# Two steps of a streaming-encoder layer joined: attention's transposes with its value products, and the scan's output products with the next chunk's first ones

## The chip, the cores and the metric

The kernel runs on one core of a Trainium2 chip. The metric is the device time of one execution in microseconds (us). Every run here is of the same program with the same inputs; a smaller time is better.

## The reference

One hybrid layer over 2048 frames of width 1024 (with 16 meta tokens ahead of them). One projection of `h` feeds two token mixers; their outputs are gated, projected, merged and normalised.

```python
(q_a, k_a, v_a, z_a, beta_a, dec_a, q_b, k_b, v_b, z_b, gate_a, gate_b) = jnp.split(h @ w_in, offsets, axis=-1)
# A: gated delta rule, a scan over chunks
v_new = u_c - w_c @ S
o_c = q_c @ S + attn_c @ v_new
S = S * gl_c + k_c.T @ v_new
# B: sliding-window attention with sinks and meta tokens, 16 heads on 4 key-value heads
scores = einsum('bkgncd,bknsd->bkgncs', q, k_w) * (SWA_HD ** -0.5) - slopes * dist
probs = softmax(concatenate([scores, sink], axis=-1), axis=-1)[..., :-1]
o = einsum('bkgncs,bknsd->bkgncd', probs, v_w)
# both are multiplied by silu(z), projected, merged with sigmoid gates, and projected again
mixed = g_a * (y_a @ w_proj_a) + g_b * (y_b @ w_proj_b)
out = layer_norm(ALPHA * h + mixed @ w_out)
```

## The kernel before, in words

The sequence is cut into four blocks of 512 frames, and `block(b)` builds the program of each. The large products are in `proj` (L311): one unit multiplies 128 rows of a weight with the block's 512 columns in 24 matmuls, because weight and input are split into a high and a low part. Every six of these matmuls the generator `proj` yields, and that is one tick.

The order of the program is written by these generators. `run(fill, streams, rates)` walks through the units; at each tick it first calls `tick()`, which issues the delayed endings that `bg` has put aside for so many ticks, and then takes at most one step of each stream whose due amount has reached 1. A rate of 1.20 therefore means one step at each tick, and 0.90 means a step at nine of ten ticks. One stream, `chain`, holds the scan of the delta rule (`stage_c` of four head pairs) and then the attention, `swa()`. The other, `side`, prepares the scan. Each engine gets its instructions in the order in which Python issues them and works them off in that order; a wait holds up all that stands behind it on that engine. The scheduler is not asked (`manual_schedule`).

The attention of a block has 16 iterations: four key-value heads by four column groups of 128 frames (two chunks each). Iteration i issues, in steps of the stream:

- `swa_front` (scores, L1105 on TensorE, 8 matmuls) of iteration i + 1; VectorE reads the scores from PSUM at L1107, two ticks later ScalarE takes exponentials (L1117), three ticks after that VectorE scales them (L1121, L1122, L1126)
- `swa_turn(0)`: four transposes of the first chunk's probabilities (L1140); ScalarE copies them out as the high part (L1142), and one tick later VectorE makes the low part (L1147)
- `late()` of iteration i - 1: `swa_vals(1)`, the four value products of the second chunk (L1156, twice L1158, L1159), and `swa_out`: ScalarE copies one half of the result out (L1164), VectorE adds the other (L1165) and multiplies it with the gate (L1169, twice)
- `swa_turn(1)`: the transposes of the second chunk
- `swa_vals(0)`: the value products of the first chunk. L1156 and L1159 read the high part, L1158 reads the low part of L1147

Each of these is a step of its own, so six large matmuls of `proj` stand between any two of them. When the last column group of a head is done, the head's result is split again (L1176 on ScalarE, L146 on VectorE). The gate and branch units of `proj` that run meanwhile have endings on VectorE too: L732 (the gate path's SiLU), L1047 (the low part of a query), L1250 (a gate times a branch).

In `stage_c` a chunk's output product (L960) is issued by a delayed ending, two ticks after the chunk's last step; the next chunk begins with L971. Products there go on with L979, L981 and L992, and VectorE's L974, L984 and L994 stand between them. L1023 is a transpose of the scan's result.

Of the kernel before, what the change touches and what calls it, by code (L numbers as in the profile page):

```python
# [15 lines left out]
AF = mybir.ActivationFunctionType  # L16
ALU = mybir.AluOpType
AX = mybir.AxisListType

P = 128  # L20
# [4 lines left out]
NC4 = TB // P  # L25
# [18 lines left out]

GS = (26, 9)
NG = 6
RATES = (0.45, 0.45, 0.45, 0.50, 1.20)
SIDE = (0.60, 0.50, 0.50, 0.55, 0.35)


# [25 lines left out]
def hybrid_kernel(  # L76
# [26 lines left out]
    V, A, G, T, SY = nc.vector, nc.scalar, nc.gpsimd, nc.tensor, nc.sync  # L103
# [26 lines left out]
    def s2(shape, dt=F32):  # L130
        return sp.tile(shape, dt, tag="s", name=nm("s"))
# [6 lines left out]
    def bank(pool=None):  # L138
        if pool is None:
            return pp.tile([P, 512], F32, tag="ps", name=nm("ps"))  # L140
        return pool.tile([P, 512], F32, tag="acc", name=nm("acc"))
# [81 lines left out]
    def until(cond):  # L223
        while not cond():
            yield
# [379 lines left out]
    def block(b, nextx):  # L605
# [337 lines left out]
        def stage_c(g):  # L943

            d, h0 = gr[g], 2 * g
            yield from until(lambda: "T" in d and "vtok" in d)
            kT, qT, ktok, vtok, attn, LT = (d[n] for n in ("kT", "qT", "ktok", "vtok", "attn", "LT"))
            sq, cj, ce = (d[n] for n in ("sq", "cj", "ce"))
            eg, neg = gates["eg"], gates["neg"]
            if first:  # L950
                yield from until(lambda: ("S", g) in meta)

            o = vtok
            so = tiny([P, 2, NC4], "so")

            def out(c, wd):
                yield 2
                pks = bank()
                for hh in range(2):
                    T.matmul(pks[:, hh * P:hh * P + P], attn[:, hh, c, :], wd[:, 0, hh, :], start=True, stop=True)  # L960
                yield 2
                V.tensor_tensor(out=o[:, :, c, :], in0=pks[:, 0:256].rearrange("p (h d) -> p h d", h=2), in1=o[:, :, c, :], op=ALU.add)
                yield 1
                for hh in range(2):
                    A.activation(junk, o[:, hh, c, :], AF.Square, accum_out=so[:, hh, c:c + 1])
                d["so", c] = True

            for c in range(NC4):
                pks = bank()
                for hh in range(2):  # L970
                    T.matmul(pks[:, hh * P:hh * P + P], kT[:, hh, c * P:(c + 1) * P], S[g][:, hh, :], start=True, stop=True)  # L971
                R = s2([P, 2, P])
                for hh in range(2):
                    V.scalar_tensor_tensor(out=R[:, hh, :], in0=pks[:, hh * P:hh * P + P], scalar=neg[:, c, h0 + hh:h0 + hh + 1],  # L974
                                           in1=vtok[:, hh, c, :], op0=ALU.mult, op1=ALU.add)
                yield
                pw = bank()
                for hh in range(2):
                    T.matmul(pw[:, hh * P:hh * P + P], LT[:, hh * NC4 + c, :], R[:, hh, :], start=True, stop=True)  # L979
                for hh in range(2):  # L980
                    T.matmul(pks[:, 256 + hh * P:256 + hh * P + P], qT[:, hh, c * P:(c + 1) * P], S[g][:, hh, :], start=True, stop=True)  # L981
                wd = s2([P, 2, 2, P])
                for hh in range(2):
                    V.tensor_scalar(out=wd[:, 1, hh, :], in0=pw[:, hh * P:hh * P + P], scalar1=ce[:, hh, c:c + 1], scalar2=None, op0=ALU.mult)  # L984
                for hh in range(2):
                    A.activation(wd[:, 0, hh, :], pw[:, hh * P:hh * P + P], AF.Copy, scale=cj[:, hh, c:c + 1])
                for hh in range(2):
                    A.activation(o[:, hh, c, :], pks[:, 256 + hh * P:256 + hh * P + P], AF.Copy, scale=eg[:, 0, c, h0 + hh:h0 + hh + 1])
                yield
                pu = bank()  # L990
                for hh in range(2):
                    T.matmul(pu[:, hh * P:hh * P + P], ktok[:, hh, c, :], wd[:, 1, hh, :], start=True, stop=True)  # L992
                for hh in range(2):
                    V.scalar_tensor_tensor(out=S[g][:, hh, :], in0=S[g][:, hh, :], scalar=eg[:, 2, c, h0 + hh:h0 + hh + 1],  # L994
                                           in1=pu[:, hh * P:hh * P + P], op0=ALU.mult, op1=ALU.add)
                bg(out(c, wd))
                yield

            def end():
                yield lambda: ("so", NC4 - 1) in d  # L1000
                V.scalar_tensor_tensor(out=so, in0=so, scalar=1.0 / P, in1=sq, op0=ALU.mult, op1=ALU.add)
                ro = tiny([P, 2, NC4], "ro")
                rsqrt_small(ro, so, [P, 2, NC4], "rs")
                for hh in range(2):
                    for c in range(NC4):
                        V.tensor_scalar(out=o[:, hh, c, :], in0=o[:, hh, c, :], scalar1=ro[:, hh, c:c + 1], scalar2=None, op0=ALU.mult)
                yield 1
                d["o"] = o
                yield from stage_y(g)

            bg(end(), 1)
# [181 lines left out]
        def swa():  # L1193

            yield from until(lambda: ("q", 1) in sr[0] and len(ld) == 2)
            swa_bias(0, ld[0][3])
            nxt = swa_front(*seqn[0], *ld.pop(0))
            yield
            late = None
            for i, (kv, cp2) in enumerate(seqn):  # L1200
                w = nxt
                if i + 2 < len(seqn):
                    ld.append(swa_load(*seqn[i + 2]))
                if i + 1 < len(seqn):
                    k2 = seqn[i + 1][0]
                    yield from until(lambda: ("q", 1) in sr[k2])
                    swa_bias(k2, ld[0][3])
                    nxt = swa_front(*seqn[i + 1], *ld.pop(0))
                    yield
                yield from until(lambda: w["n"])  # L1210
                swa_turn(0, w)
                yield
                if late is not None:
                    late()
                    yield
                swa_turn(1, w)
                yield
                yield from until(lambda: ("p", 0) in w and ("ok", "zs", 1) in sr[kv])
                w["pO"] = bank()
                swa_vals(0, w)  # L1220
                yield

                def late(kv=kv, cp2=cp2, w=w):
                    swa_vals(1, w)
                    swa_out(kv, cp2, w)

            yield from until(lambda: ("p", 1) in w)
            late()
            yield
# [298 lines left out]
```

## Time and profile before

| what | value |
|---|---|
| median of 3 runs | 2648.5 us (2647.66 to 2649.97) |
| profiled execution, its own time | 2648.3 us |
| its span, first to last instruction | 2646.5 us |
| TensorE matmul busy (PE) | 2608.6 us, 99% |
| VectorE (DVE) / ScalarE (ACT) / GpSimd (POOL) busy | 58% / 46% / 29% |
| mean granted TensorE clock | 0.998 |

The busy time of an engine is the time in which at least one of its instructions runs; for TensorE matmuls overlap, so the distance from one start to the next says what a matmul costs, and not its duration. PEld is TensorE's loading of weights, which lies beside the matmuls. The granted clock is the share of full speed that the chip's throttle allows: 1.00 is 2.4 GHz, 0.50 is 1.2 GHz. A row of the timeline has its start in us, how long it took, the engine, the line, the operation, out<-in, and how many instructions are merged; in square brackets stands how long the engine was idle before it, and who ended that.

### The profile page before, as it was taken

Reading aid. Unit: us, or ns where it says so; the run is one execution under the profiler, and the core shown is the slowest. Engines: PE = TensorE matmul, PEld = TensorE weight load, DVE = VectorE, ACT = ScalarE, POOL = GpSimd, SP = SyncE. Lnnn points to the kernel's source line nnn. Section 1 sums busy time; section 2 is a strip of 40 time slices with the busy share of each in tenths; the row PEclk is TensorE's granted clock in tenths of the full one; section 3 lists DMA queues with packets and bytes.
Section 4 is the critical chain, followed back from the end, with each engine's and each line's share of the span. In section 5 each row is a group of like instructions: output and inputs, shape, how many; then the busy total and the mean of one; then the engine's idle time right before and its main releaser. Section 6 shows DMA issues by size and latency. Waiting matters only on the chain.

```text
span 2646.5 us, 44333 instructions
## 1 busy us (share of the span) xinstructions
PE 2608.6 (99%) x15444; PEld 2173.8 (82%) x15444; DVE 1533.4 (58%) x3863; ACT 1222.9 (46%) x3260; POOL 772.8 (29%) x1792
## 2 busy tenths in 40 slices
PE   9999999999999999999999999999999999999998
PEld 7677878888888888888888888888888888888886
DVE  6667756763565554763465554676347456476435
ACT  4565545552245544653224554565323454365422
POOL 2554333532056330111116532010102753011022
PEclk9999999999999999999999999999999999999999
DMA  7655555653675454674466545476347644557533
GB/s 257 207 198 180 186 191 159 200 167 96 205 244 169 135 167 143 201 207 132 152 225 186 170 135 164 151 212 184 120 157 243 190 142 149 164 172 210 171 98 136
DMA packets 243136, 461.61 MB, mean 174 GB/s; under 512 B 77648, under 2 KB 135760, under 8 KB 242912
## 3 DMA queue, kind: packets, MB, share of 16 engines
q1 hardware_dynamic: 242912, 458.78, 54.4%
q8 instruction: 122, 2.00, 0.3%
q14 instruction: 102, 0.84, 0.1%
HBM read 379.87 MB, written 78.81 MB: 173 GB/s over the span
## 4 chain that ended last, share of the span: by engine, by line
PE 89%; DVE 6%; ACT 3%; DMA 1%; issue 1%; SPq 0%; POOL 0%; DVEq 0%; ACTq 0%
PE acc L311 63%; PE ps L1140 2%; PE ps L1105 2%; PE ps L915 1%; PE ps L960 1%; PE ps L807 1%; PE ps L971 1%; PE ps L1158 1%; PE ps L992 1%; PE acc L1408 1%; PE acc L1411 1%; PE acc L1410 1%; PE ps L979 1%; PE ps L981 1%; PE ps L1408 1%; PE ps L1411 1%
## 5 line engine op out<-in xcount | busy, mean ns | idle before, releaser
L311 PE MATMUL acc<-xh,wh 128*128 128x512 f32 x1800 | 735.2, 408 | 0.3 <-ACT wh L275 0.3
L311 PE MATMUL acc<-xl,wh 128*128 128x512 f32 x1800 | 705.4, 392 | 0.0
L311 PE MATMUL acc<-xh,wl 128*128 128x512 f32 x1800 | 480.7, 397 | 0.0
L275 ACT ACTIVATE wh<-wr 128x1024 fp32r<-128x1024 f32 (+1 forms) x246 | 258.4, 1050 | 281.6 <-PE acc L311 151.8
L311 PEld LDWEIGHTS acc<-xh,wh 128*128 128x128 f32 x1800 | 339.1, 188 | 60.1 <-issue 1.4
L311 PEld LDWEIGHTS acc<-xl,wh 128*128 128x128 f32 x1800 | 339.7, 189 | 57.1
L311 PEld LDWEIGHTS acc<-xh,wl 128*128 128x128 f32 x1800 | 329.1, 189 | 65.6 <-issue 0.5
L718 DVE SCALAR_TENSOR_TENSOR s<-st,cw,s 128x512 f32<-128x512 f32 x288 | 229.4, 797 | 108.2 <-ACT st L713 101.2
L311 PE MATMUL acc<-y,wh 128*128 128x512 f32 x1024 | 251.5, 392 | 0.0
L146 DVE TENSOR_TENSOR wl<-wr,wh 128x1024 fp32r<-128x1024 f32 (+2 forms) x125 | 161.9, 1295 | 149.7 <-ACT wh L275 128.6
L841 POOL TENSOR_TENSOR tm<-X,g 128x60 f32<-128x60 f32 (+24 forms) x496 | 163.1, 329 | 251.8 <-DMA g<-d 216.7
L311 PEld LDWEIGHTS acc<-y,wh 128*128 128x128 f32 x1024 | 188.5, 188 | 36.7
L311 PE MATMUL acc<-xh,wr 128*128 128x512 f32 x624 | 210.7, 402 | 0.0
L1257 POOL TENSOR_TENSOR g<-g 128x512 f32<-128x512 f32 x32 | 69.7, 2177 | 395.4 <-DVE g L1250 385.5
L843 POOL TENSOR_TENSOR X<-X,tm 128x60 f32<-128x60 f32 (+24 forms) x496 | 170.8, 344 | 38.8
L1142 ACT ACTIVATE s<-ps 104x512 fp32r<-104x512 f32 (+2 forms) x128 | 76.3, 597 | 153.3 <-PE ps L1140 137.3
L1250 DVE SCALAR_TENSOR_TENSOR g<-g,acc 128x512 f32<-128x512 f32 x64 | 44.0, 687 | 154.5 <-PE acc L311 154.5
L311 PEld LDWEIGHTS acc<-xh,wr 128*128 128x128 f32 x624 | 115.6, 188 | 21.5
L311 PE MATMUL acc<-y,wl 128*128 128x512 f32 x512 | 130.7, 392 | 0.0
L146 POOL TENSOR_TENSOR wl<-wr,wh 128x256 fp32r<-128x256 f32 x120 | 87.0, 756 | 137.4 <-ACT wh L275 116.6
L760 POOL TENSOR_TENSOR g<-cm,gh 128x256 fp32r<-128x256 f32 x64 | 53.9, 872 | 249.6 <-DVE gh L672 206.9
L1241 ACT ACTIVATE g<-acc,bg__162 128x512 f32<-128x512 f32 x64 | 44.1, 689 | 177.3 <-PE acc L311 171.0
(340 smaller groups left out, 4679.6 us busy)
## 6 DMA issues: line engine op xcount, KB each, us to landing
wr<-in_wfm_dram SPq DMA_DIRECT2D x214, 512.0 KB
wl<-ws SPq DMA_DIRECT2D x165, 512.0 KB
wr<-ws SPq DMA_DIRECT2D x78, 512.0 KB
wh<-ws SPq DMA_DIRECT2D x75, 512.0 KB
ws<-wl SPq DMA_DIRECT2D x68, 512.0 KB
g<-kd SPq DMA_DIRECT2D x240, 96.0 KB
ws<-wh SPq DMA_DIRECT2D x38, 512.0 KB
wr<-in_wo_dram SPq DMA_DIRECT2D x32, 512.0 KB
```

The source lines that it names most:

```text
L146: eng.tensor_tensor(out=out_, in0=src, in1=f(hi), op=ALU.subtract)
L275: A.activation(hi[:, k], raw[:, k], AF.Copy)
L311: T.matmul(ps, w_[:, k, :], r_(k), start=(n == 0), stop=(n == 3 * NK - 1))
L718: V.scalar_tensor_tensor(out=acc, in0=st[:, 3 - d:TB + 3 - d], scalar=cw[:, s, 3 - d:4 - d], in1=acc, op0=ALU.mult, op1=ALU.add)
L760: G.tensor_tensor(out=gt[:, hh, c:c + 2], in0=tri.unsqueeze(1).to_broadcast([P, 2, P]), in1=part[:, c:c + 2, h0 + hh:h0 + hh + 1].to_broad ...
L841: G.tensor_tensor(out=tm[:, :n, :r], in0=X[:, :n, j:j + 1].to_broadcast([P, n, r]), in1=L[:, j:j + 1, j + 1:].to_broadcast([P, n, r]), op= ...
L843: G.tensor_tensor(out=X[:, :n, j + 1:], in0=X[:, :n, j + 1:], in1=tm[:, :n, :r], op=ALU.add)
L1105: T.matmul(o_, d["q", rt][:, 2 * cp2 + ch], KX[:, l, ch, s:208], start=l == 0, stop=l == 1)
L1140: T.transpose(out=pT[0:kt, j * 256 + rt * P:j * 256 + rt * P + P], in_=Pt[:, ch, rt, s + j * kt:s + j * kt + kt], identity=ident)
L1142: A.activation(ph[0:kt], pT[0:kt], AF.Copy)
L1257: G.tensor_tensor(out=m[:, u % 2, :], in0=t[:, 0, :], in1=t[:, 1, :], op=ALU.add)
L1408: T.matmul(acc, ah, wl[:, k2, :], start=False, stop=kq == 3 and k2 == 1)
```

## The change

Four things are edited. In `swa()`, `late()` no longer yields on either side: it follows `swa_turn(0)` in the same step. `swa_turn(1)` moves behind the wait for the first chunk's low part and into the step of `swa_vals(0)`. An iteration so has three steps instead of five. The rate of `chain` in the stage in which attention runs goes from 1.20 to 0.90. And in `stage_c` the output product of chunk c - 1 is issued right behind chunk c's first products instead of two ticks after the chunk's last step; what VectorE and ScalarE do with it stays in a delayed ending.

```diff
-RATES = (0.45, 0.45, 0.45, 0.50, 1.20)
+RATES = (0.45, 0.45, 0.45, 0.50, 0.90)
...
             def out(c, wd):
-                yield 2
-                pks = bank()
+                po = bank()
                 for hh in range(2):
-                    T.matmul(pks[:, hh * P:hh * P + P], attn[:, hh, c, :], wd[:, 0, hh, :], start=True, stop=True)
-                yield 2
-                V.tensor_tensor(out=o[:, :, c, :], in0=pks[:, 0:256].rearrange("p (h d) -> p h d", h=2), in1=o[:, :, c, :], op=ALU.add)
-                yield 1
-                for hh in range(2):
-                    A.activation(junk, o[:, hh, c, :], AF.Square, accum_out=so[:, hh, c:c + 1])
-                d["so", c] = True
-
+                    T.matmul(po[:, hh * P:hh * P + P], attn[:, hh, c, :], wd[:, 0, hh, :], start=True, stop=True)
+
+                def end():
+                    yield 2
+                    V.tensor_tensor(out=o[:, :, c, :], in0=po[:, 0:256].rearrange("p (h d) -> p h d", h=2), in1=o[:, :, c, :], op=ALU.add)
+                    yield 1
+                    for hh in range(2):
+                        A.activation(junk, o[:, hh, c, :], AF.Square, accum_out=so[:, hh, c:c + 1])
+                    d["so", c] = True
+
+                bg(end())
+
+            wd = None
             for c in range(NC4):
                 pks = bank()
                 for hh in range(2):
                     T.matmul(pks[:, hh * P:hh * P + P], kT[:, hh, c * P:(c + 1) * P], S[g][:, hh, :], start=True, stop=True)
+                if c:
+                    out(c - 1, wd)
                 R = s2([P, 2, P])
...
-                bg(out(c, wd))
                 yield
+            out(NC4 - 1, wd)
...
                 swa_turn(0, w)
-                yield
                 if late is not None:
                     late()
-                    yield
-                swa_turn(1, w)
                 yield
                 yield from until(lambda: ("p", 0) in w and ("ok", "zs", 1) in sr[kv])
+                swa_turn(1, w)
                 w["pO"] = bank()
                 swa_vals(0, w)
                 yield
```

The new lines shift the numbers: behind `stage_c` a line of the kernel before has a number that is six higher in the changed one (L1140 is L1146 there, L1147 is L1153, L1156 to L1159 are L1162 to L1165, L1164 is L1170, L1165 is L1171, L1169 is L1175). An iteration of the second block on TensorE, before; `cm` is the identity of a transpose, `acc` the bank of a large product, and the L1156 to L1159 in the middle write `ps_12068`, the bank of the iteration before:

```order
L1140 MATMUL ps_12135<-cm,g_11970 104x128 x4
L311 MATMUL acc_12148<-xh_7832,wh_12036 128x512
...
L1156 MATMUL ps_12068<-s_12058,s_10885 128x4x64
L1158 MATMUL ps_12068<-s_12066,s_10885 64x4x64 x2
L1159 MATMUL ps_12068<-s_12058,s_10885 128x4x64
L311 MATMUL acc_12148<-xh_7870,wh_12036 128x512
...
L1140 MATMUL ps_12181<-cm,g_11970 104x128 x4
L311 MATMUL acc_12148<-xh_7950,wh_12036 128x512
...
L1156 MATMUL ps_12196<-s_12140,s_11780 128x4x64
L1158 MATMUL ps_12196<-s_12164,s_11780 64x4x64 x2
```

The same iteration on TensorE in the changed kernel, where `s_12162` and `s_12179` are the high and the low part of the transposes in `ps_12157`:

```order
L1146 MATMUL ps_12157<-cm,g_11998 104x128 x4
L1162 MATMUL ps_12066<-s_12064,s_10885 128x4x64
L1164 MATMUL ps_12066<-s_12077,s_10885 64x4x64 x2
L1165 MATMUL ps_12066<-s_12064,s_10885 128x4x64
L311 MATMUL acc_12137<-xh_7870,wh_12019 128x512
...
L311 MATMUL acc_12137<-xl_7907,wh_12019 128x512
L1146 MATMUL ps_12181<-cm,g_11998 104x128 x4
L1162 MATMUL ps_12188<-s_12162,s_11804 128x4x64
L1164 MATMUL ps_12188<-s_12179,s_11804 64x4x64 x2
L1165 MATMUL ps_12188<-s_12162,s_11804 128x4x64
```

From the first transposes to the product that reads their low part there were three gaps of six large matmuls; one gap is left. VectorE in the same iteration, before; `s_12164` is the low part of the first chunk's transposes, `s_12170` the sum of the iteration before:

```order
L1047 SCALAR_TENSOR_TENSOR g_12131<-acc_12040,g_12131 64x8x64 x2
L1147 TENSOR_TENSOR s_12164<-ps_12135,s_12140 104x512
L1165 TENSOR_TENSOR s_12170<-ps_12068,s_12170 64x512
L1169 TENSOR_TENSOR g_11202<-s_12170,g_11202 64x2x128 x2
L1147 TENSOR_TENSOR s_12194<-ps_12181,s_12186 104x512
```

And VectorE in the changed kernel, with the first chunk's low part in `s_12179`:

```order
L1053 SCALAR_TENSOR_TENSOR g_12125<-acc_12023,g_12125 64x8x64 x2
L1171 TENSOR_TENSOR s_12168<-ps_12066,s_12168 64x512
L1175 TENSOR_TENSOR g_11202<-s_12168,g_11202 64x2x128 x2
L1153 TENSOR_TENSOR s_12179<-ps_12157,s_12162 104x512
L1153 TENSOR_TENSOR s_12199<-ps_12181,s_12186 104x512
```

The sum and the two gate products of the iteration before now stand ahead of the first chunk's low part on VectorE. In the scan, the first place on TensorE where the order differs (first block; - is before, + the change):

```order
-L960 MATMUL ps_2251<-s_2160,g_915 128x128 x2
 L311 MATMUL acc_2238<-xh_116,wh_2136 128x512
 L311 MATMUL acc_2238<-xl_117,wh_2136 128x512
...
-L971 MATMUL ps_2289<-S_85,g_565 128x128 x2
-L791 MATMUL ps_2295<-cm,g_2287 128x128 x4
+L975 MATMUL ps_2286<-S_85,g_565 128x128 x2
+L959 MATMUL ps_2289<-s_2160,g_915 128x128 x2
```

The output product of the first chunk (L960, L959 in the change) moved behind the second chunk's first product.

## Rows read from the trace of the kernel before

**Rows 1.** The page: busy us by engine, then the chain that ended last.
```profile
PE 2608.6 (99%) x15444; PEld 2173.8 (82%) x15444; DVE 1533.4 (58%) x3863; ACT 1222.9 (46%) x3260; POOL 772.8 (29%) x1792
...
PE 89%; DVE 6%; ACT 3%; DMA 1%; issue 1%; SPq 0%; POOL 0%; DVEq 0%; ACTq 0%
```
**Rows 2.** Windows: pure projection, then the second block's attention; clock behind POOL.
```profile
600.00:670.00 70.00, 70.00 (x310) 57.96 (x310) 26.20 (x26) 18.95 (x20) 14.74 (x7) 1.00 0.37 121
1068.00:1204.00 136.00, 135.35 (x756) 114.59 (x755) 95.15 (x301) 81.26 (x205) 15.40 (x70) 1.00 0.67 200
```
**Rows 3.** Waits of TensorE: us in total, times, longest.
```profile
PE ps L992 <- DVE s L984: 3.1, 3, 1.0
PE ps L1158 <- DVE s L1147: 2.6, 5, 1.6
...
PE ps L1140 <- DVE g L1126: 1.4, 5, 0.3
...
PE ps L1023 <- DVE s L1147: 1.1, 3, 0.4
```
**Rows 4.** Timeline of one attention iteration in the second block.
```profile
1127.86 0.39 PE L311 MATMUL acc<-xl,wh 128*128 128x512 f32 x1
...
1128.09 0.60 PE L1140 MATMUL ps<-cm,g 128*104 128x128 f32 x4
...
1128.73 0.60 ACT L1142 ACTIVATE s<-ps 104x512 fp32r<-104x512 f32 x1 [3.91 <-PE ps L1140]
1128.77 0.39 PE L311 MATMUL acc<-xl,wh 128*128 128x512 f32 x1
...
1129.92 0.28 PE L1156 MATMUL ps<-s,s 104*128 104x256 f32 x1
1130.04 0.40 PE L1158 MATMUL ps<-s,s 104*64 104x256 f32 x2
1130.27 0.28 PE L1159 MATMUL ps<-s,s 104*128 104x256 f32 x1
1130.39 0.40 PE L311 MATMUL acc<-xh,wh 128*128 128x512 f32 x1
...
1131.25 0.60 ACT L1164 ACTIVATE s<-ps 64x512 f32<-64x512 f32 x1
...
1131.79 0.60 PE L1140 MATMUL ps<-cm,g 128*104 128x128 f32 x4
1131.88 0.68 DVE L1165 TENSOR_TENSOR s<-ps,s 64x512 f32<-64x512 f32 x1 [1.60 <-ACT s L1164]
...
1132.60 0.85 DVE L1169 TENSOR_TENSOR g<-s,g 64x256 f32<-64x256 f32 x2
...
1133.48 0.69 DVE L1147 TENSOR_TENSOR s<-ps,s 104x512 fp32r<-104x512 f32 x1
...
1139.95 0.28 PE L1159 MATMUL ps<-s,s 104*128 104x256 f32 x1
```
**Rows 5.** VectorE's other work in this stretch, groups by line.
```profile
L146 DVE TENSOR_TENSOR y<-g,y 128x1024 fp32r<-128x1024 f32 x48 | 59.0, 1229 | 4.4 <-PE ps L1140 3.8 <-ACT wh L275 0.4
L1047 DVE SCALAR_TENSOR_TENSOR g<-acc,g 64x512 fp32r<-64x512 f32 x64 | 44.1, 690 | 17.7 <-ACT g L1043 16.5
L1250 DVE SCALAR_TENSOR_TENSOR g<-g,acc 128x512 f32<-128x512 f32 x64 | 44.0, 687 | 154.5 <-PE acc L311 154.5
```
**Rows 6.** Timeline of the first block's first iteration, a window behind it, one in the scan.
```profile
432.96 0.68 DVE L1147 TENSOR_TENSOR s<-ps,s 40x512 fp32r<-40x512 f32 x1
...
433.70 0.59 PE L1158 MATMUL ps<-s,s 40*64 40x256 f32 x2 [1.62 <-DVE s L1147]
...
434.43 2.93 PE L311 MATMUL acc<-xh,wl 128*128 128x512 f32 x6
...
434.00:435.00 1.00, 1.00 (x4) 0.70 (x3) 0.83 (x6) 0.00 (x0) 0.20 (x2) 0.50 1.07 360
...
908.00:912.00 4.00, 2.96 (x16) 2.21 (x15) 2.96 (x6) 1.60 (x5) 0.00 (x0) 1.00 0.40 133
```

## The prediction, made before the changed kernel ran

> **What bounds the kernel now.** I read the page first: TensorE is busy for 2608.6 of the span of 2646.5 us, and 89% of the chain that ended last is its own [rows 1]. The reader is to see that time can change in two ways only: TensorE gets other work, or it waits more or less. The change leaves the number of instructions alone, so only waits count. The next view, the stretch of the second block's attention, shows how little there is to win there: TensorE is busy for 135.35 of 136.00 us, VectorE for 95.15 and ScalarE for 81.26 [rows 2]. The list of TensorE's waits says the same: L1158 waits 2.6 us in total for L1147, L1140 1.4, L1023 1.1 for L1147, and L992 in the scan 3.1 [rows 3].
>
> The last view is one iteration, row by row [rows 4]. Three gaps of six large matmuls hide the chain of small steps between TensorE, ScalarE and VectorE there; that is why hardly anything waits.
>
> **The steps joined in attention.** What lies between the transposes and the product that reads their low part? In the kernel before, VectorE makes the low part (L1147) ahead of the sum and the gate products of the iteration before (L1165, L1169), and TensorE has three gaps to pass. In the change it makes it behind them, and TensorE has one gap. I set the need against the cover, both from T, the start of the last value product of the iteration before (L1159, at 1130.27 in [rows 4]).
>
> The cover, what TensorE does until it stands at L1158: 0.12 us to the next large matmul (1130.27 to 1130.39), 1.40 us for six of them (to the transposes at 1131.79), 0.44 us for four transposes and 0.12 us from L1156 to L1158 (1129.92 to 1130.04). The 0.44 us come from 1127.86 to 1128.77: 0.91 us for two large matmuls at 0.23 us each with four transposes between them, so 0.45, and I take 0.44. Sum: T + 2.08 us.
>
> The need: L1159 ends at T + 0.28, so ScalarE can take L1164 at T + 0.31. It has the copy L1142 of the new transposes ahead of it; this starts 0.64 us behind the transposes' start (1128.09 to 1128.73) and takes 0.60, and the transposes start 0.79 us ahead of T (0.44 for themselves, 0.35 from 1129.92 to 1130.27). So L1142 ends at T + 0.45, and L1164 starts between T + 0.31 and T + 0.47. From there the very sequence that the change sets up already stands in the trace once: L1164 at 1131.25, L1165 at 1131.88, L1169 at 1132.60, L1147 at 1133.48 with 0.69 us, so 2.92 us without a wait inside [rows 4]. TensorE then goes on 0.06 us later: L1147 ended at 433.64, L1158 started at 433.70 [rows 6]. Sum: T + 3.29 to T + 3.45.
>
> TensorE thus waits 1.21 to 1.37 us at L1158; I take 1.30. Of the 15 iterations of a block that have a predecessor, the order of the changed kernel leaves one gap of six in 14, and two gaps in one, where 1.40 us more cover it. 4 blocks x 14 x 1.30 = **73 us** (68 to 77).
>
> **What else stands ahead of L1147.** In three iterations of a block the split of a finished head (L146, 1.23 us) and in one or two another ending (L1250 or L732, about 0.69 us) now stand between L1169 and L1147 on VectorE [rows 5]. They add to the wait: 4 x (3 x 1.23 + 1.5 x 0.69) = **19 us**; at the low end half of it, 9, where VectorE gets to them in time. In two early iterations of a block a pair of L1047 (2 x 0.69 us) and the scaling of the next scores stand ahead of L1165: 0 to 8 us, I take **4**.
>
> **What the waits do to the clock.** In the first block's first iteration L1158 waited 1.62 us for L1147. Right behind it the granted clock was 0.50, that is 1.2 GHz, and six large matmuls took 2.93 us [rows 6] where 1.40 to the next kind is usual [rows 4]. So a long wait can cost about 1.5 us more. The longest wait of the scan, 1.0 us at L992 [rows 3], lies in the window from 908 to 912 us, and there the clock stays at 1.00 [rows 6]. Of the new waits those with L146 in them, 12 at 2.5 us, are longer than 1.62 us. I charge half of them: **10 us** (0 to 18). The Trainium skill ("Perfetto Trace Analysis", section "Matmul Optimizations") says that the matmul engine scales its power with utilization, and that matmuls should therefore run back to back in batches. By it, a step that joins two small groups should do no harm; the trace agrees on the first half only, with the 2.93 us behind a wait.
>
> **What comes back.** The waits at L1158, L1140 and L1023 (2.6 + 1.4 + 1.1 us) may go, with the 1.5 us of the one slow stretch, 6.6 us at most. The first iteration, where most of it lies, has no predecessor and keeps two gaps; I take **-3**. The joined groups save a change of shape 128 times; from 0.45 us for four inserted transposes against 4 x 0.11, that is 0.01 us each, **-1**.
>
> **At no cost.** The rate: before, 1.20 already meant one step per tick, so the steps slow down by a tenth but are three instead of five. Attention has 384 large matmuls among it per block and not 492, and the 108 others (25 us) follow behind. There TensorE runs without a pause, 70.00 of 70.00 us [rows 2], so moving them costs nothing; if cover were lacking there, its price would be that of the attention stretch. The keys' loads are issued one iteration ahead; an iteration lasts 9.68 us now (1130.27 to 1139.95 in [rows 4]) and in the forecast 9.68 - 7 x 0.23 + 1.3 = 9.4, so the lead stays; no row of L1105 waits for a transfer now [rows 3]. In the scan the output product moves behind L971 within the same tick or the next. It gives L974 0.45 us more cover and takes as much from L994, where nothing waits today; the price lies within the 3.1 us of L992, plus or minus, and I take 0.
>
> **The sum.** 73 + 19 + 4 + 10 - 3 - 1 = 102 us. The profiled execution took 2648.3 us (median of the three runs: 2648.5), so **2750 us**.
>
> **The rivals.**
> - *The clock falls at nearly every wait.* For it: the row at 434.43. Against it: waits of 1.0 us did nothing. 56 x 1.5 us in place of 10 give 74 more: 2825 us.
> - *A smaller loss.* If only about half of the iterations have to wait, because ScalarE and VectorE are ahead there, 28 x 1.30 + 9: 2690 us. Against it: the chain starts from TensorE's own L1159, so nothing can be ahead of it.
> - *No change.* The waits stay hidden if the need is below 2.08 us. That takes 1.2 us off the 3.3, for instance L1147 ahead of L1165 on VectorE; the order of the change has it behind. Then 2648 - 1 to 2650.
> - *Faster.* One mechanism: L1158 finds its low part ready as in the middle of [rows 4], and the waits and slow clock of the first iterations go. 6.6 + 1 us: 2641 us. It decides if VectorE reaches L1147 before T + 2.08; it needs a second gap of six between the groups, which the order has in one iteration of fifteen.
>
> **How the numbers follow.** Forecast (2700 to 2795) 0.70, smaller loss (2655 to 2700) 0.08, clock at nearly every wait (2795 to 2850) 0.10, no change 0.05, faster 0.07. The range from 2690 to 2815 holds the first whole and the near parts of the two beside it, a little over 0.8. Its lower bound is also the sum of the low ends (68 + 9 + 0 + 0 - 7 - 1 = 69, so 2717) less a share for the smaller loss; its upper the high ends (77 + 19 + 8 + 18 - 0 = 122, so 2770) and half of the clock rival. A measurement of this kernel can tell about 0.2%, some 5 us, from no change: slower 0.88, the same 0.05, faster 0.07.
>
> **What would show it.** In the profile of the changed kernel L1164 (the L1158 of before) waits for L1153 (L1147) some 60 times, 1.2 to 1.4 us mostly and 2.5 us where L146 stands ahead; TensorE's busy share in the attention stretch falls from 99% to some 82% (102 / 4 = 25 us of waits and slow clock in a stretch that keeps its 136 us); VectorE waits for ScalarE ahead of L1171 (L1165) as it does now; the granted clock falls to 0.50 for a few us behind some of them. Behind attention, 720 large matmuls run without a pause. The prediction is wrong if these waits are not there or are short, if they are all followed by the slow clock, or if waits in the scan (L992's place) grow by more than a few us.

## The result and the profile after

The changed kernel takes 2851.0 us (median of 4 runs, 2847.4 to 2851.6); the kernel before took 2648.1 us beside it (2644.7 to 2650.0). The ratio is 1.0763, with a 95% interval from 1.0747 to 1.0779. The change costs 203 us; the forecast was a loss of 102, and 2851 us lies above its range. The direction and the main place were right, the size was half.

The page of the changed kernel: busy us by engine, then TensorE's busy share and its granted clock in 40 slices of the span.

```profile
PE 2661.6 (93%) x15444; PEld 2206.2 (77%) x15444; DVE 1530.3 (54%) x3863; ACT 1224.0 (43%) x3260; POOL 774.2 (27%) x1792
...
PE   9999997789999999779999999878999999978998
...
PEclk9999998999999999999999999999999999999999
```

The number of instructions is that of before [rows 1]. TensorE's digits now fall to 7 and 8 in four places, the attention stretches of the four blocks. Its list of waits (us in total, times, longest) answers to [rows 3]:

```profile
PE ps L1164 <- DVE s L1153: 108.9, 59, 4.5
PE ps L1146 <- DVE g L1132: 37.0, 25, 7.1
PE ps L1162 <- ACT s L1148: 7.6, 10, 1.3
...
PE ps L998 <- DVE s L990: 3.1, 3, 1.0
PE ps L1029 <- DVE g L1012: 2.7, 1, 2.7
```

L1164 is the old L1158, the product that reads the low part: 2.6 us have become 108.9. L1146, the transposes (L1140 before), waits 37.0 us for the scaling of the scores, for which the forecast charged nothing. The scan's L998 (L992) waits as before. The whole attention stretch of the second block, from its first scores to its last value product, as a window (columns as in [rows 2]):

```profile
1113.47:1296.17 182.70, 146.20 (x779) 120.41 (x778) 109.72 (x357) 88.40 (x236) 18.16 (x82) 0.95 0.49 146
```

It lasts 182.7 us with 384 large matmuls in it, and TensorE is idle for 36.5 of them. Before, the same stretch lasted 160.6 us with 492 large matmuls and 0.8 us idle:

```profile
1050.86:1211.45 160.59, 159.77 (x888) 134.97 (x887) 110.89 (x360) 94.20 (x243) 17.83 (x82) 1.00 0.65 194
```

**An account that closes.** Three terms give the loss in the profiled execution (span 2849.6 against 2646.5, so 203.1 us). The gaps of TensorE over 0.05 us add up to 174.4 us against 25.3: 149.1. It worked for 85.0 us at a granted clock of 0.50, waits left out, against 3.4; half of the difference is lost: 40.8. And each wait costs 0.17 us more than its gap, because the last record ahead of it runs for 0.40 us where the next matmul would start after 0.23: 127 waits against 42, 14.5 us. Sum: 204.4. The same account closes to 3.3 us or better for each of the fifteen kernels below, so to within these 3 us nothing but waits and the clock moves the time here.

**The chain of the forecast.** TensorE, VectorE and ScalarE of the changed kernel in one iteration, timeline:

```profile
1199.54 0.28 PE L1165 MATMUL ps<-s,s 104*128 104x256 f32 x1
...
1200.20 0.59 ACT L1170 ACTIVATE s<-ps 64x512 f32<-64x512 f32 x1
...
1200.83 0.68 DVE L1171 TENSOR_TENSOR s<-ps,s 64x512 f32<-64x512 f32 x1 [1.30 <-ACT s L1170]
1201.05 0.60 PE L1146 MATMUL ps<-cm,g 128*104 128x128 f32 x4
...
1201.54 0.85 DVE L1175 TENSOR_TENSOR g<-s,g 64x256 f32<-64x256 f32 x2
...
1202.41 0.69 DVE L1153 TENSOR_TENSOR s<-ps,s 104x512 fp32r<-104x512 f32 x1
...
1203.15 0.45 PE L1164 MATMUL ps<-s,s 104*64 104x256 f32 x2 [1.38 <-DVE s L1153]
```

Read it by the releasers: L1165 ends, ScalarE copies (L1170), VectorE adds and multiplies (L1171, L1175), only then makes the low part (L1153), and TensorE has stood since its one gap was over. That is the forecast's T + 3.29 to 3.45, here 3.6.

**What the forecast did not have.** An iteration where two gaps lie between the scores and the transposes:

```profile
1208.77 0.69 ACT L1245 ACTIVATE g<-acc,bg__162 128x512 f32<-128x512 f32 x1 [4.50 <-PE acc L311]
...
1209.36 0.46 ACT L1123 ACTIVATE g<-g,mn 128x208 f32<-128x208 f32 x1
1209.36 0.28 PE L1165 MATMUL ps<-s,s 104*128 104x256 f32 x1
...
1211.16 0.20 ACT L1125 ACTIVATE m<-m 128x4 f32<-128x4 f32 x1
1211.26 0.58 ACT L1148 ACTIVATE s<-ps 104x512 fp32r<-104x512 f32 x1
...
1211.87 0.59 ACT L1170 ACTIVATE s<-ps 64x512 f32<-64x512 f32 x1
...
1212.49 0.68 DVE L1171 TENSOR_TENSOR s<-ps,s 64x512 f32<-64x512 f32 x1 [3.76 <-ACT s L1170]
...
1214.84 0.45 PE L1164 MATMUL ps<-s,s 104*64 104x256 f32 x2 [2.56 <-DVE s L1153]
```

L1165 starts at 1209.36, yet its copy L1170 only 2.5 us later: the four exponentials and L1125 of the next scores, issued two ticks behind these, stand ahead on ScalarE from 1209.36 to 1211.36. Of the 59 waits at L1164, 18 have exponentials ahead of L1170; they are the 18 that are longer than 2.5 us, 51.7 us in all (2.87 each). In 15 of them L1170 starts 1.8 to 3.4 us behind L1165. In the other three (2.65 us each) it starts only 0.8 us behind, and the split L146 (1.23 us), which stands ahead of L1153 on VectorE, does more than the exponentials; four of the 15, the longest with 3.7 to 4.5 us, have both. The other 41 waits come to 57.2 us, 1.39 each: 28 with nothing between L1175 and L1153 on VectorE, 1.30 us on average, five with L146, 2.35 each, and eight with another ending (L732 or L1254), 1.13 on average.

**The clock.** Behind a wait of 3.70 us, large matmuls in the timeline:

```profile
1191.74 0.45 PE L1164 MATMUL ps<-s,s 104*64 104x256 f32 x2 [3.70 <-DVE s L1153]
...
1193.23 0.63 PE L311 MATMUL acc<-xh,wh 128*128 128x512 f32 x1
...
1193.66 0.63 PE L311 MATMUL acc<-xl,wh 128*128 128x512 f32 x1
```

And a window over them:

```profile
1192.80:1196.20 3.40, 3.40 (x9) 2.61 (x9) 0.84 (x4) 0.00 (x0) 0.00 (x0) 0.51 0.69 167
```

The granted clock is 0.51 there, and they start every 0.43 us in place of 0.23.

### The profile page after: what moved, and what is told of

The parts are those of the page before. It is cut to its first block, busy times and chain, and to the rows that moved or that the text cites. A ratio compares the mean times of both kernels' runs of the same rounds, so it can differ in the third digit from the quotient of the medians.

```text
span 2849.6 us, 44348 instructions
## 1 busy us (share of the span) xinstructions
PE 2661.6 (93%) x15444; PEld 2206.2 (77%) x15444; DVE 1530.3 (54%) x3863; ACT 1224.0 (43%) x3260; POOL 774.2 (27%) x1792
## 5 line engine op out<-in xcount | busy, mean ns | idle before, releaser
L311 PE MATMUL acc<-xl,wh 128*128 128x512 f32 x1800 | 717.2, 398 | 0.0
L311 PEld LDWEIGHTS acc<-xh,wh 128*128 128x128 f32 x1800 | 345.1, 192 | 62.8 <-issue 1.0
L311 PEld LDWEIGHTS acc<-xl,wh 128*128 128x128 f32 x1800 | 346.3, 192 | 60.5
L311 PEld LDWEIGHTS acc<-xh,wl 128*128 128x128 f32 x1800 | 336.5, 192 | 67.7 <-issue 0.5
L146 DVE TENSOR_TENSOR wl<-wr,wh 128x1024 fp32r<-128x1024 f32 (+2 forms) x125 | 162.2, 1298 | 161.6 <-ACT wh L275 142.7
L1254 DVE SCALAR_TENSOR_TENSOR g<-g,acc 128x512 f32<-128x512 f32 x64 | 44.0, 688 | 224.0 <-PE acc L311 223.8
L1113 DVE CUSTOM_DVE_ANT_0 g<-ps,g,nsnk 128x208 f32<-128x208 f32 (+2 forms) x256 | 94.6, 425 | 121.9 <-PE ps L1111 71.2
L1245 ACT ACTIVATE g<-acc,bg__162 128x512 f32<-128x512 f32 x64 | 44.1, 689 | 264.4 <-PE acc L311 236.7
L1164 PE MATMUL ps<-s,s 104*64 104x256 f32 (+2 forms) x256 | 54.6, 295 | 108.9 <-DVE s L1153 108.9
L146 POOL TENSOR_TENSOR wl<-wr,wh 128x256 fp32r<-128x256 f32 x120 | 88.2, 766 | 188.8 <-ACT wh L275 150.2
```

The costliest lines, as they stand in the source:

```text
L146: eng.tensor_tensor(out=out_, in0=src, in1=f(hi), op=ALU.subtract)
L311: T.matmul(ps, w_[:, k, :], r_(k), start=(n == 0), stop=(n == 3 * NK - 1))
L1113: V.tensor_tensor_reduce(out=Pt[:, ch, rt, s:208], in0=pS[:, rt * 256 + s:rt * 256 + 208], in1=bias[:, ch, rt, s:208], scale=1.0, scalar=n ...
L1164: T.matmul(o_[0:64], VX[0:kt, ch, j, 0:64], pl[0:kt, j * 256:j * 256 + 256], start=False, stop=False)
L1245: A.activation(gt_[u][:, br, :], ps, AF.Tanh, scale=0.5, bias=bg_[:, 8 * br + u:8 * br + u + 1])
L1254: V.scalar_tensor_tensor(out=t[:, br, :], in0=t[:, br, :], scalar=1.0, in1=ps, op0=ALU.add, op1=ALU.mult)
```

## The experiments

Times are medians; "lost" is against the kernel before on the same chip. Line numbers are those of the kernel that is told of. The three terms of the account, in us, for the change and its parts:

| kernel | lost | waits | clock | 0.17 each |
|---|---|---|---|---|
| change | 203 | 149 | 41 | 14 |
| scan edit alone | 36 | 29 | 7 | 0 |
| rate alone | 13 | 10 | 1 | 0 |
| first joint alone | 91 | 73 | 5 | 15 |
| second joint alone | 90 | 70 | 10 | 9 |
| change without the scan edit | 192 | 141 | 35 | 15 |

**1. The scan edit alone.** The changed kernel with the attention and the rate of before:

```diff
-RATES = (0.45, 0.45, 0.45, 0.50, 0.90)
+RATES = (0.45, 0.45, 0.45, 0.50, 1.20)
...
                 swa_turn(0, w)
+                yield
                 if late is not None:
                     late()
+                    yield
+                swa_turn(1, w)
                 yield
                 yield from until(lambda: ("p", 0) in w and ("ok", "zs", 1) in sr[kv])
-                swa_turn(1, w)
                 w["pO"] = bank()
```

> The scan's edit alone: output product behind the next chunk's first product, attention and its rate (1.20) as before. My theory: the whole loss of 203 us sits in attention, so 2643 to 2653 us, within about 0.2% of before, and TensorE's waits in the list keep their sizes (L992's place about 3 us). Rival: the moved output product holds up the scan and carries part of the loss: over 2660 us, with new waits at the places of L960, L971 or L979.

Measured: 2685.2 us, ratio 1.0138 [1.0123, 1.0153]. My theory fell, and the time is the rival's. It is not lost in the scan, though, where the rival had it: the scan's waits are those of before, and the list has one new row, 32.3 us of L1146 waiting for L1132, at the first transposes of each block's attention. Timeline of this kernel there:

```profile
1071.40 0.30 ACT L966 ACTIVATE junk<-g 128x128 f32<-128x128 f32 x1
...
1072.25 0.17 DVE L1007 SCALAR_TENSOR_TENSOR so<-so,sq 128x8 f32<-128x8 f32 x1 [4.09 <-ACT junk L966]
...
1074.67 1.66 DVE L1012 TENSOR_SCALAR g<-g,ro 128x128 f32<-128x128 f32 x8
...
1076.65 1.04 DVE L1132 TENSOR_SCALAR g<-g,ls 128x208 f32<-128x208 f32 x4
...
1077.03 1.12 PE L1146 MATMUL ps<-cm,g 128*104 128x128 f32 x4 [7.45 <-DVE g L1132]
```

The kernel before, VectorE, the same place (its L1126 is the scaling, L1001 to L1006 the norm):

```profile
1059.67 1.04 DVE L1126 TENSOR_SCALAR g<-g,ls 128x208 f32<-128x208 f32 x4
...
1064.20 0.15 DVE L1001 SCALAR_TENSOR_TENSOR so<-so,sq 128x8 f32<-128x8 f32 x1
...
1066.61 1.66 DVE L1006 TENSOR_SCALAR g<-g,ro 128x128 f32<-128x128 f32 x8
```

The ending of a chunk took five ticks before (2 + 2 + 1) and takes three now. So the closing norm of the scan comes two ticks earlier, and on VectorE it passes the scaling of attention's first scores. There it first stands for 4.09 us, because ScalarE has eight exponentials ahead of the squares L966 that it needs, then works 4.1 us, and TensorE waits behind both.

**2. The norm three ticks later, all groups**, on top of 1, in the scan's closing `end()`:

```diff
                 yield lambda: ("so", NC4 - 1) in d
+                yield 3
```

> The scan edit alone, with the scan's closing norm issued three ticks later, so that VectorE has it behind the first scaling of attention's scores, where it stood before the change. Theory (the 36 us of the scan edit alone are this norm's place on VectorE and the low clock behind the wait): the wait of 7.4 us at the first transposes of each block goes, 2645 to 2655 us. Rival (the output product's new place in the scan costs too): 2665 us or more.

Measured: 2657.7 us, ratio 1.0036 [1.0024, 1.0049]. The waits at the first transposes are gone (2.0 us left at L1147), so the mechanism holds; 10 us remain, between the two expectations. The list names L791, 12.6 us in 7 waits for L723: in the other three groups the delayed norm now stands ahead of L723.

**3. The same for the last group only.**

```diff
+                if g == 3:
+                    yield 3
```

> The scan edit alone, with the closing norm three ticks later in the last group of heads only, the one that runs into attention. Theory (the 10 us left with the norm late in all four groups are the norms of the other three, which then stand ahead of the convolution's last step and the transposes that wait for it): 2644 to 2652 us. Rival (they are the output product's new place in the scan): 2655 us or more.

Measured: 2652.8 us, ratio 1.0018 [1.0009, 1.0027], 0.8 us above the theory's bound; L791 is back at 1.5 us. Some 4.5 us stay, 3.2 of them in the clock's term. That is at the bound of what can be told from no change. So the output product's new place costs next to nothing, and the norm that it pulls along costs nearly all of the 36.

**4. The rate alone**, in the kernel before.

```diff
-RATES = (0.45, 0.45, 0.45, 0.50, 1.20)
+RATES = (0.45, 0.45, 0.45, 0.50, 0.90)
```

> The kernel before with the rate of 0.90 alone. Theory (the rate costs nothing where three gaps cover the chain): 2643 to 2654 us. Rival (a lower rate moves attention's steps against the projections and opens waits of its own): over 2660 us.

Measured: 2661.4 us, ratio 1.0047 [1.0035, 1.0060]. The rival by a little: 10 us of new waits, most of them in the first block, whose attention idles for 11.1 us (2.9 before). The longest there are 1.9 and 2.0 us at L1140.

**5. The change without the scan edit**: joints and rate as in the change, the scan's end as before.

```diff
             for c in range(NC4):
...
-                if c:
-                    out(c - 1, wd)
...
+                bg(out(c, wd))
                 yield
-            out(NC4 - 1, wd)
```

> The change in attention and the rate of 0.90, with the scan of before. Theory (the scan edit costs one long wait at the first transposes of each block's attention, with the low clock behind it): that wait (7.1 and three of 3.2 us) goes, and 2815 to 2838 us. Rival (what the scan edit costs alone is hidden once attention's steps are joined): within 5 us of the changed kernel, 2846 to 2856.

Measured: 2839.7 us, ratio 1.0722 [1.0704, 1.0739]: 11 us less than the change, just outside the theory's 2815 to 2838. With the rate of 0.90 attention begins a tick later against the projections. In the second block ScalarE then starts the exponentials 6.3 us before TensorE reaches the transposes (2.9 us in 1), and VectorE stands for the squares for 1.26 us in place of 4.09. So in blocks two to four the norm costs a wait of 3.2 us in place of 7.4; part of the scan edit's price is hidden so.

**6. The low part ahead on VectorE**, `late()` moved into the second step of the changed kernel:

```diff
                 swa_turn(0, w)
-                if late is not None:
-                    late()
                 yield
                 yield from until(lambda: ("p", 0) in w and ("ok", "zs", 1) in sr[kv])
+                if late is not None:
+                    late()
                 swa_turn(1, w)
```

> The changed kernel with the earlier iteration's value products (late) moved out of the first transposes' step into the step of the second transposes, so that VectorE makes the first chunk's low part ahead of the sum and the gate products. Still three steps, rate 0.90 and one gap of six large matmuls. Theory (the order on VectorE makes the wait): need from the transposes' start 0.64 + 0.60 + 0.69 + 0.06 = 1.99 us against a cover of 0.44 + 1.40 + 0.47 + 0.44 + 0.12 = 2.87 us, so the waits for the low part fall from 109 us to under 25, and the time to 2715 to 2760 us. Rival (one gap is too short or attention is too dense whatever the order): the waits stay above 80 us and the time above 2800 us.

Measured: 2753.0 us, ratio 1.0396 [1.0380, 1.0411], as the theory had it; 98 us come back with three steps and one gap as in the change. The edit moves the products and copies of `late()` too, so it does not tell VectorE's order from ScalarE's. L1164's waits fall from 108.9 to 9.3 us, L1146's rise from 37.0 to 60.8:

```profile
PE ps L1146 <- DVE g L1132: 60.8, 43, 7.1
PE ps L1164 <- DVE s L1153: 9.3, 22, 1.5
```

**7. A second gap**, one more `yield` between the two joined steps:

```diff
                 if late is not None:
                     late()
                 yield
+                yield
```

> The changed kernel with one gap of six large matmuls more between the step that issues the first transposes and the one that reads their low part; the joined steps stay as they are. Theory (the missing gap is the price): the waits of TensorE at the value products for the low part fall from 108.9 us to under 25, the low clock behind them goes with them (half of some 100 us at 1.2 GHz), 2715 to 2765 us. Rival (the joined step itself is the price, because it asks ScalarE and VectorE for too much at once): the waits stay over 60 us, 2800 us or more.

Measured: 2721.6 us, ratio 1.0278 [1.0264, 1.0292]. L1164's waits are 9.2 us, the theory again: 130 us come back, and the joined steps are as they were. L1146's waits are 52.3 us, 15 more than in the change:

```profile
PE ps L1146 <- DVE g L1132: 52.3, 36, 7.1
PE ps L1164 <- DVE s L1153: 9.2, 13, 1.8
```

**8. A lower rate** in the changed kernel.

```diff
-RATES = (0.45, 0.45, 0.45, 0.50, 0.90)
+RATES = (0.45, 0.45, 0.45, 0.50, 0.60)
```

> The changed kernel with the rate 0.60 in place of 0.90: three steps take five ticks, so an iteration has as many large matmuls (30) as before, but between the first group and the second there is still one gap of six. Theory (chain against one gap): the wait for the low part is still there in some 56 iterations with 1.2 us or more, 70 to 110 us in total, while the waits of the first transposes for the scaling go; 2735 to 2790 us. Rival (attention is too dense, VectorE and ScalarE cannot follow three steps at that pace): with the old density the waits go, under 2670 us.

Measured: 2875.0 us, ratio 1.0846 [1.0827, 1.0864], worse than either theory. The attention stretch has 486 large matmuls (474 in the first block), nearly the 492 of before, but the additional ones do not lie between the two joined steps, where the order still has one gap. L1164 waits 116.9 us, 28 times with the exponentials ahead (18 in the change), because two gaps now follow each set of scores. The clock costs 70 us in place of 41. So it is not how densely attention is packed, but where the gaps lie.

**9. The exponentials a tick later**, the scaling where it was:

```diff
-                yield 2
+                yield 3
                 for ch in range(2):
...
-                yield 3
+                yield 2
                 V.tensor_tensor(out=ls, in0=ls, in1=m2, op=ALU.add)
```

> The changed kernel with the exponentials issued three ticks behind the scores in place of two, and the scaling two ticks behind them in place of three, so the scaling stays where it is. The exponentials then stand behind the copies of the transposes and of the values on ScalarE, where they stood ahead of them in the iterations with two gaps. Theory: the 30 waits for the low part that are longer than 1.6 us (76 of the 109 us) lose what the exponentials add, about 1.1 us each, and the 8 us at the first value product go; 2790 to 2820 us. Rival (the long waits come from VectorE's own queue): no change, 2840 us or more.

Measured: 2811.1 us, ratio 1.0613 [1.0597, 1.0629]. No wait at L1164 has the exponentials ahead now, and 2 are over 2.5 us where there were 18; 22 us of waits and 15 us of clock come back.

**10 and 11. One joint alone**, in the kernel before with its rate of 1.20: `late()` in the step of `swa_turn(0)`, or `swa_turn(1)` in the step of `swa_vals(0)`.

```diff
                 swa_turn(0, w)
-                yield
                 if late is not None:
                     late()
-                    yield
+                yield
                 swa_turn(1, w)
```

> The kernel before with one joint alone: the first transposes and the last values of the iteration before in one step. Theory (what counts are the gaps between the transposes and the product that reads their low part, and here one of three goes): two gaps still cover the chain in nearly all iterations, waits for the low part under 20 us, some at the scaling of the scores since an iteration has a step less; 2655 to 2705 us. Rival (each joint costs half of what both cost): 2735 us or more.

```diff
-                swa_turn(1, w)
-                yield
                 yield from until(lambda: ("p", 0) in w and ("ok", "zs", 1) in sr[kv])
+                swa_turn(1, w)
                 w["pO"] = bank()
```

> The kernel before with the other joint alone: the second transposes and the first values in one step. Theory: as for the first joint alone, two gaps are left, 2655 to 2705 us. Rival (each joint costs half of what both cost): 2735 us or more.

Measured: 2738.9 us, 1.0347 [1.0333, 1.0361], and 2738.4 us, 1.0339 [1.0325, 1.0354]. The rival's number came, by another way than halving: with two gaps the low part is nearly covered (second joint 4.2 us). What waits is L1140 for L1126. Waits of the kernel with the first joint:

```profile
PE ps L1140 <- DVE g L1126: 54.4, 64, 2.0
PE ps L1158 <- DVE s L1147: 23.2, 33, 1.6
```

The scaling is issued a fixed 2 + 3 ticks behind the scores, and the transposes that read it come one step after the next iteration's scores. An iteration of five steps so left a tick between the two; an iteration of four issues both in one tick, and TensorE stands for the scaling itself, 0.8 us mostly. (The expectations of 12 and 13 count one more in both cases.)

**12. First joint, scaling a tick earlier.**

```diff
                 A.activation(m2, m2, AF.Exp)
-                yield 3
+                yield 2
```

> The kernel before with the first joint alone and the scaling of the scores one tick nearer to the exponentials (2 ticks in place of 3). Theory (an iteration has five steps now, and the scaling, due five ticks behind the scores, is issued in the very tick of the transposes that read it): TensorE's waits there fall from 54.4 us to under 15, 2665 to 2700 us. Rival (VectorE itself comes late, its work does not fit a shorter iteration): these waits stay over 30 us, 2715 us or more.

Measured: 2676.5 us, ratio 1.0102 [1.0087, 1.0117]; the same list:

```profile
PE ps L1158 <- DVE s L1147: 22.3, 30, 2.6
PE ps L1140 <- DVE g L1126: 5.9, 8, 1.3
```

54.4 us became 5.9 and 62 us came back: it was the fixed delay, not a VectorE short of time.

**13. First joint, transposes released a tick later.**

```diff
+                yield 1
                 w["n"] = 1
```

> The kernel before with the first joint alone and the transposes released one tick behind the scaling; an iteration that has caught up with its scaling thus gets its sixth tick back. Theory (the same fixed delay): waits at the scaling under 15 us, those for the low part at most the 23 us of the first joint alone, 2655 to 2690 us. Rival (VectorE is late): 2715 us or more.

Measured: 2729.1 us, ratio 1.0299 [1.0282, 1.0316]. The wait for the scaling went as expected (6.1 us), but that for the low part rose from 23.2 to 57.5 us and the time is the rival's. Every second iteration now has two gaps behind its scores. In 9 of these waits the exponentials stand ahead of the copy, 18.4 us in all. Four more, one of 6.2 and three of 3.1 us, 15.4 in all, are the scan's closing norm, which now stands on VectorE between the first transposes of a block and their low part:

```profile
1097.75 1.66 DVE L1006 TENSOR_SCALAR g<-g,ro 128x128 f32<-128x128 f32 x8
...
1100.19 0.45 PE L1159 MATMUL ps<-s,s 104*64 104x256 f32 x2 [3.07 <-DVE s L1148]
```

The other 23.7 us are about what the first joint alone had (23.2). So the tick took the wait for the scaling away and opened two others; that the scaling itself comes late it does not show.

**14. The change with three causes taken away:** 7, 13 and 3 together.

> The changed kernel with its three causes of waiting taken away and the joined steps kept: a second gap ahead of the product that reads the low part, one tick more between the scaling of the scores and the transposes that read it, and the closing norm of the scan's last group three ticks later. Theory (these are all that the change costs): waits for the low part and for the scaling under 15 us together, 2645 to 2675 us. Rival (the joined steps cost something of their own, or the clock falls for another reason than long waits): 2690 us or more.

Measured: 2702.8 us, ratio 1.0208 [1.0192, 1.0223]. The waits for the scaling are down to 2.5 us, those for the low part are 44.1 in 38 waits, with two gaps, where the second gap alone had 9.2. Ten of the 38 (17.4 us) have the exponentials ahead of the copy, twelve (15.1 us) the split L146 on VectorE. The time is the rival's: my list was not complete. A wait that is mended by a tick moves the exponentials and endings of the neighbours, and another one opens.

**15. The same with 6 in place of 7.**

> The changed kernel with the ending of the iteration before moved into the second step, so that VectorE has the low part ahead of it, with the transposes released one tick behind the scaling and the closing norm of the scan's last group three ticks later. Theory (order on VectorE, fixed delay and norm are the three causes): waits for the low part and the scaling under 20 us together, 2650 to 2690 us. Rival (a cause is missing from the list): 2700 us or more.

Measured: 2689.8 us, ratio 1.0153 [1.0138, 1.0168], at the theory's upper end; the waits for low part and scaling are 25 us, not under 20. No version with a joint came near the kernel before; the best is the one with the first joint alone and the scaling earlier, 28 us behind.

## Why the prediction was half right

**Right: the main mechanism.** "TensorE thus waits 1.21 to 1.37 us at L1158" is what the 28 waits with nothing else in their chain show, 1.30 us on average. The queue on VectorE was counted rightly too: twelve waits have the split L146 ahead of L1153, three in a block, and eight another ending. The low part put ahead, or a second gap, takes nearly all of it away (6 and 7). That it would be neither "no change" nor "faster" was right too.

**Undersized: what stands ahead of the low part.** Forecast 73 + 19 + 4; measured 106.3 us more at L1164 than before, and some 9 us for the 54 new waits at 0.17. The missing 20 us and the longest waits come from ScalarE. The step that failed is "L1164 starts between T + 0.31 and T + 0.47" (L1170 in the change): it had only the copy ahead of it, and not the exponentials. In the 15 iterations where they delay it most, the copy starts between T + 1.8 and T + 3.4. The trace of the kernel before could have told, in the very iteration of [rows 4], between two of its rows:

```profile
1129.22 0.46 ACT L1117 ACTIVATE g<-g,mn 128x208 f32<-128x208 f32 x1
...
1131.03 0.19 ACT L1119 ACTIVATE m<-m 128x4 f32<-128x4 f32 x1
```

There L1164 starts at 1131.25, T + 0.98, right behind the exponentials of the next scores, and they stand ahead of it in 56 of the 64 iterations of that kernel. The gaps hid this, so no wait showed it. The forecast took the row at 1131.25 as the start of a chain and did not ask why it was that late; its "nothing can be ahead of it" fails for the same reason. Experiment 9, which moves the exponentials, shows their price in the change.

**Failed: "The waits at L1158, L1140 and L1023 (2.6 + 1.4 + 1.1 us) may go", taken as -3.** L1140 did not go, it rose by 35.6 us. I counted the steps of an iteration for the low part and not for the scaling, which is due a fixed number of ticks behind the scores (10 and 12 show that for one joint). In the change some 17 of the 37 us are the scan's norm at the first transposes, one of 7.1 and three of 3.2 us.

**Failed: "In the scan ... I take 0" and "The rate".** The products were nearly free (4.5 us are left in 3), but the edit also shortens the ending by two ticks, and the work that follows it moved past a waiting engine's work: 36 us alone, 11 in the change. I looked at the queue that the product is moved past, TensorE's, and not at VectorE's. The rate costs 13 us alone, since in the first block not all is covered.

**Failed: the clock, "10 us (0 to 18)".** 41 us. Without the exponentials ahead (9) 15 of them go, so a good part follows from the long waits that the forecast did not have. The rival "the clock falls at nearly every wait" has a number (2825) nearer to the measured one, but not the mechanism: in the change the clock fell behind 3 of the 35 waits from 1.0 to 1.6 us. The Trainium skill ("Perfetto Trace Analysis", section "Matmul Optimizations") advises to run matmuls back to back in batches. Joining small groups did not serve that end here: the mean granted clock is 0.982 where it was 0.998, because of the waits that the joining opened.

**Open.** Why in 8 the clock fell behind 24 of 24 waits between 2.45 and 3.3 us and in the change behind 14 of 19 is not settled; nor are the last 40 to 55 us of 14 and 15, wait by wait. The second gap of 7 together with the earlier scaling of 12 was not run.

## What to carry to other kernels

Joining steps of an interleaved stream saves no work; it removes the cover that other work gave to the chains between the engines, so count the gaps for every chain that runs through the step, not only for the one that is edited. Read from the trace of the kernel before what stands ahead of each link of such a chain, also where no wait shows it yet: spare cover hides it. Delays that are counted in ticks keep their length when an iteration gets shorter: ask of each what is now issued in the same tick. And an edit that takes a step out of an ending moves all that follows the ending, so compare the order on the engines where those followers run, not on the one where the edit stands.

## What the hardware showed

The clock's price depends strongly on how long one wait is. Over the changed kernel and the fifteen others, a stretch at 0.50 began within a wait or up to 3.5 us behind it for 6 of 258 waits from 1.0 to 1.6 us, 42 of 120 from 1.6 to 2.45, 74 of 93 from 2.45 to 3.3, and all 30 above, the kernel's start left out. Such a stretch lasted 3.4 to 10.2 us. In 1 the clock fell while TensorE still waited (from 1072.3, the wait ended at 1077.0), so 4.7 of its 10.2 us cost nothing; in 10 some 90 new waits of mostly 0.3 to 1 us, 73 us in all, cost only 5 us of clock, where the four of 7.1 to 7.4 us in 1 cost 7. Few long waits are dearer than many short ones of the same sum.
